# Ordering GpSimd's low parts behind VectorE's combinations in a differential-attention encoder layer

## The chip, the cores and the metric

The kernel runs on one core of one Trainium2 chip. The metric is the device time of one execution in microseconds. Times of the trace count from the start of the profiled span. The engines are TensorE (PE; its weight loads are PEld), VectorE (DVE), ScalarE (ACT), GpSimd (POOL) and SyncE (SP), which issues most transfers.

## The reference, cut to what matters

One layer of an encoder over 2048 positions of width 1024: a norm and one input projection, differential attention with 4 heads beside a recurrent group, an output projection, and a gated feed-forward part. The change touches the attention alone:

```python
sc = einsum('bqhcd,bkhcd->bhcqk', qb, kh) * scale        # c = 0, 1: two score maps per head, 64 wide
sc = sc - slopes[:, None, None, None] * dist              # distance bias
p = softmax(sc, axis=-1)
w = p[:, :, 0] - lam * p[:, :, 1]                         # the two maps are combined
o = einsum('bhqk,bkhe->bqhe', w, vh)                      # 128 wide values
o = rms_norm(o, subln_g) * (1.0 - lambda_init)
```

## The kernel before

Attention (`phase2`) runs over 4 heads of 16 query tiles, 128 queries each. One call of `step(n, cur)` (lines 550 to 597) issues the work of tile n (`cur`) together with later stages of earlier tiles: b1, b2 and b3 are tiles n-1, n-2 and n-3, and two tiles make a pair (`Pair`), whose stages come 4 (`pv`), 6 (`nrm`) and 8 (`fin`) steps behind its first tile. `nrm` and `fin` exist in even steps only. The order of instructions on TensorE, VectorE, ScalarE and GpSimd is the order in which `step` writes them (a manual schedule); each engine runs its queue in order.

In a step:

- `scores(hf)` (line 407): 12 matmuls into two PSUM tiles `sc`, one for each score map c, for half hf of the 2048 keys. The two tiles are used again by the next half.
- `biased(c, hf)` (line 411): VectorE's score pass, which adds the bias from PSUM to `e[c]` in SBUF and keeps the minimum. `softmax(c)` (line 416): ScalarE's exponential over 2048 columns.
- `combine(hf)` (line 427): VectorE's combination, e0 = e1 * rc + e0 over 1024 columns, both inputs in SBUF. There are two of these in a step.
- `transposed(i)` (lines 433, 442): TensorE turns a quarter of the combined tile (`tp`), ScalarE copies it to SBUF: quarter 0 to `wn`, quarter 1 to `wf`, quarters 2 and 3 to `wg`.
- `parts(i)` (line 448, by the helper `split`, lines 72 to 77): the fp32 values are split into a high part `wTh` (ScalarE, a rounding copy) and a low part `wTl` (GpSimd, value minus high part). `parts(1)` does `wf` (512 columns), `parts(2)` does `wg` (1024 columns).
- `values(part)` (lines 465 and 80 to 82): TensorE's products with the values, into `pv`. In an even step parts 0 and 1 of a pair, in an odd step parts 2 and 3. Part 0 uses `wn` alone, the others `wTh` and `wTl`.
- For the norm of a pair: with part 3 of the values ScalarE copies `pv` to `o` (line 472) and GpSimd squares it (`osq`, line 474) and the sums of the softmax (line 476). In the following even step TensorE adds the squares up (`norm_sums`, line 481, into `nrm_ps`), VectorE scales the sums (`norm_scale`, line 486), GpSimd takes a power and spreads it over 128 columns (`rr`, `rb`, lines 488 and 491). In the even step after that TensorE turns `rb` (`norm_spread`, line 497) and VectorE applies it (`scaled`, line 500).

In the last head GpSimd also makes low parts of the output weights (`load_out`, line 516), four times.

Of the kernel before, what the change touches and what calls it, by code (L numbers as in the profile page):

```python
# [9 lines left out]
F32 = mybir.dt.float32  # L10
# [3 lines left out]
AF = mybir.ActivationFunctionType  # L14
ALU = mybir.AluOpType
# [3 lines left out]
P = 128  # L19
# [10 lines left out]
EPS = 1e-6  # L30
# [12 lines left out]
def encoder_layer(ctx, tc, x, w_qkr, w_v, w_out, w_up, w_down, w_a, w_x, par, lams, g_attn, g_ffn, g_fin, out):  # L43
    nc = tc.nc
    V, A, G, T = nc.vector, nc.scalar, nc.gpsimd, nc.tensor

    def pool_of(name, **kw):
        return tc.tile_pool(name=name, reuse_waits="tile", **kw)
# [18 lines left out]
    mhalf = const.tile([P, 4], F32, name="mhalf")  # L67
# [4 lines left out]
    def split(hi, lo, src, hi_eng=A, lo_eng=V):  # L72
        if hi_eng is A:
            A.activation(out=hi, in_=src, func=AF.Copy)  # L74
        else:
            hi_eng.tensor_copy(hi, src)
        lo_eng.tensor_tensor(out=lo, in0=src, in1=hi, op=ALU.subtract)  # L77

    def mm3(ps, lh, ll, rh, rl, first, last):
        T.matmul(ps, lh, rh, start=first, stop=False)  # L80
        T.matmul(ps, lh, rl, start=False, stop=False)  # L81
        T.matmul(ps, ll, rh, start=False, stop=last)  # L82
# [243 lines left out]
    def phase2(kp):  # L326
        es = ExitStack()
        hip = es.enter_context(pool_of("ah", bufs=2))
        sm = es.enter_context(pool_of("asm", bufs=3))
# [10 lines left out]
        PQ = 2 * P  # L340
        NQ = 1

        ones = cp.tile([P, P], F32, name="ones")
# [15 lines left out]
                        op0=ALU.mult)  # L359
# [28 lines left out]
        class Tile:  # L388
# [35 lines left out]

            def combine(self, hf):
                e0, e1 = [e[:, hf * 1024:(hf + 1) * 1024] for e in self.e]
                V.scalar_tensor_tensor(out=e0, in0=e1, scalar=self.rc, in1=e0, op0=ALU.mult, op1=ALU.add)  # L427

            def transposed(self, i):

# [13 lines left out]
            def parts(self, i):  # L444

                j = self.t % 2
                dst = (slice(None), slice(0, 4) if i == 1 else slice(4, 12), slice(j * P, (j + 1) * P))
                split(self.pair.wh[dst], self.pair.wl[dst], self.wf if i == 1 else self.wg, lo_eng=G)

        class Pair:  # L450

# [8 lines left out]
            def values(self, part):  # L460
                if part == 0:
                    self.pv = ps_v.tile([P, PQ], F32, name="pv", tag="pv")
                for kt in range(part * 4, part * 4 + 4):
                    if part < NQ:
                        T.matmul(self.pv, self.vs[2][:, kt, :], self.wn[:, kt, :], start=kt == 0, stop=False)  # L465
                    else:
                        m = kt - 4 * NQ
                        mm3(self.pv, self.vs[0][:, kt, :], self.vs[1][:, kt, :], self.wh[:, m, :], self.wl[:, m, :],
                            kt == 0, kt == NT - 1)
                if part == 3:  # L470
                    self.o = sm.tile([P, PQ], F32, name="o", tag="o", bufs=3)
                    A.activation(out=self.o, in_=self.pv, func=AF.Copy)
                    self.sq = sm.tile([P, PQ], F32, name="osq", tag="osq", bufs=1)
                    G.tensor_tensor(out=self.sq, in0=self.o, in1=self.o, op=ALU.mult)
                    self.s2 = sm.tile([P, 2], F32, name="s2", tag="s2")
                    G.tensor_tensor(out=self.s2, in0=self.s0, in1=self.s0, op=ALU.mult)

            def norm_sums(self):
                self.ssp = nrm_ps[:, PQ:PQ + 4]
# [2 lines left out]

            def norm_scale(self):

                e0 = sm.tile([P, 2], F32, name="se", tag="se")
                V.scalar_tensor_tensor(out=e0, in0=self.s2, scalar=EPS * P, in1=self.ssp[:, 0:4:2], op0=ALU.mult, op1=ALU.add)
                r = sm.tile([P, 2], F32, name="rr", tag="rr")
                G.tensor_tensor(out=r, in0=e0, in1=mhalf[:, 0:2], op=ALU.pow)
                self.rb = sm.tile([P, 2, P], F32, name="rb", tag="rb", bufs=1)
                for j in range(2):  # L490
                    G.tensor_scalar(out=self.rb[:, j, :], in0=ones, scalar1=r[:, j:j + 1], scalar2=None, op0=ALU.mult)

            def norm_spread(self):

# [55 lines left out]
        def step(n, cur):  # L550

            b1 = tiles[n - 1] if 0 <= n - 1 < last else None
            b2 = tiles[n - 2] if 0 <= n - 2 < last else None
            pair = lambda lag: pairs[(n - lag) // 2] if n >= lag and (n - lag) // 2 < len(pairs) else None
            pv, nrm, fin = pair(4), pair(6), pair(8)
            if n % 2:
                nrm = fin = None
            b3 = tiles[n - 3] if 0 <= n - 3 < last else None
            if cur:
                cur.scores(0)  # L560
            if b1:
                b1.softmax(1)
            if cur:
                cur.biased(0, 0)
                cur.biased(1, 0)
            if b2:
                b2.transposed(0)
                b2.transposed(1)
                b2.parts(1)
            if b3:  # L570
                b3.parts(2)
            if pv:
                pv.values(n % 2 * 2)
            if fin:
                fin.norm_spread()
            if b1:
                b1.ratio()
                b1.combine(0)
            if cur:
                cur.scores(1)  # L580
                cur.biased(0, 1)
                cur.biased(1, 1)
            if b2:
                b2.transposed(2)
                b2.transposed(3)
            if cur:
                cur.softmax(0)
            if pv:
                pv.values(n % 2 * 2 + 1)
            if nrm:  # L590
                nrm.norm_sums()
            if b1:
                b1.combine(1)
            if fin:
                fin.scaled()
            if nrm:
                nrm.norm_scale()

        ordered = {mybir.EngineType.PE, mybir.EngineType.DVE, mybir.EngineType.Activation, mybir.EngineType.Pool}
        ks, vs = load_head(0)  # L600
# [13 lines left out]
        for h in range(NH):  # L614
            for t in range(NT):
                if t % 4 == 0:
                    qs = qs_next
                if t % 2 == 0:
                    pairs.append(Pair(h, t // 2, vs))
                tiles.append(Tile(h, t, qs, ks, pairs[-1]))  # L620
                step(n, tiles[n])
                if t % 4 == 1:
                    if t + 4 < NT:
                        qs_next = load_q(h, t // 4 + 1)
                    elif h + 1 < NH:
                        nxt = load_head(h + 1)
                        qs_next = load_q(h + 1, 0)
                        load_values(h + 1, nxt[1])
                if t == NT - 1 and h + 1 < NH:
                    sum_values(nxt[1])  # L630
                if h == NH - 1 and t in (6, 8, 10, 12):
                    raw = fetch_out(t // 2 + 1)
                if h == NH - 1 and t in (7, 9, 11, 13):
                    load_out(t // 2 + 1, t // 2 - 3, G, raw)
                n += 1
            if h + 1 < NH:
                ks, vs = nxt
# [3 lines left out]
        while n < last + 10:  # L641
            step(n, None)
            early.run(n - last)
            if n == last + 1:
                load_two((0, 1), (1, 2))
            if n == last + 4:
                load_two((2, 0), (3, 3))
            n += 1
# [671 lines left out]
    kp_stack = ExitStack()  # L1320
    kp = kp_stack.enter_context(pool_of("kp", bufs=2, side="right"))
    wo, x0 = phase2(kp)
    sl = Slots()
    sl.add(ctx.enter_context(pool_of("ba", bufs=1)), [f"b{i}" for i in range(9)])
# [75 lines left out]
```

## Time and profile before

| | |
|---|---|
| time, median of 3 runs | 2679.63 us (2678.31 to 2682.24) |
| profiled execution, its own time | 2677.01 us |
| its span | 2675.2 us |
| TensorE busy | 2580.4 us (96%) |
| VectorE busy | 1978.8 us (74%) |
| ScalarE busy | 1340.7 us (50%) |
| GpSimd busy | 574.9 us (21%) |
| mean granted clock of TensorE | 0.985 |

Busy shares are means over stages with different limits. Attention takes the span from about 520 to 1135 us; what bounds it is read from its own stretch, from the timelines of single engines and from the chain of work that ended last, in which each piece is followed back to what released it. TensorE's matmuls overlap in the timeline, and their ends are modelled; the chain shows them end to end. An operation of VectorE or GpSimd that is held shows as a longer record, not as idle time.

### The profile page before, as it was taken

The page shows a single profiled execution, that of the slowest core. Times are in us where ns is not written, and L with a number is a line of the kernel's source. Part 1 is how long each engine was busy: PE and PEld are TensorE (multiplying, and loading weights), DVE is VectorE, ACT ScalarE, POOL GpSimd, SP SyncE. Part 2 cuts the span into 40 slices and gives each one's busy share as a digit, 9 for nine tenths or more (in the row PEclk, how much of TensorE's full clock was granted, in tenths as well). Part 3 has the DMA queues.
Part 4 walks back from the last instruction along what each step waited for, and adds up shares of the span by engine and source line. Part 5 has one row for each costly group of instructions (what it writes and reads, how often), then busy time and mean ns, then how long its engine had stood idle before and what let it go on. Part 6 is the DMA issues. An engine that isn't in the chain of part 4 may idle for free.

```text
span 2675.2 us, 33375 instructions
## 1 busy us (share of the span) xinstructions
PE 2580.4 (96%) x12904; PEld 2098.3 (78%) x12904; DVE 1978.8 (74%) x2453; ACT 1340.7 (50%) x1730; POOL 574.9 (21%) x467
## 2 busy tenths in 40 slices
PE   8999999989999999999999999989999999899898
PEld 6878778768888888787778888878888877678686
DVE  5454554699999999644488888897777787765876
ACT  4343543678888888632344444454444453322432
POOL 1013313346666766700000000000000001000000
PEclk9999999989999999999999999999999999999999
DMA  5421221320202001344443434343333337554543
GB/s 190 129 85 60 81 79 64 130 93 17 87 23 87 25 25 38 99 149 138 169 165 118 154 122 143 129 161 126 123 122 124 115 108 177 130 147 98 148 144 126
DMA packets 141391, 297.60 MB, mean 111 GB/s; under 512 B 17904, under 2 KB 73968, under 8 KB 133552
## 3 DMA queue, kind: packets, MB, share of 16 engines
q1 hardware_dynamic: 134416, 272.55, 29.9%
q0 software_dynamic: 6240, 21.24, 4.2%
q8 instruction: 101, 1.65, 0.3%
q10 hardware_dynamic: 576, 1.69, 0.2%
q14 instruction: 58, 0.48, 0.1%
HBM read 177.98 MB, written 117.44 MB: 110 GB/s over the span
## 4 chain that ended last, share of the span: by engine, by line
PE 69%; DVE 6%; issue 2%; POOL 1%; ACT 1%; DMA 0%; POOLq 0%; SPq 0%; DVEq 0%; ACTq 0%
PE q L977 44%; PE sc L407 7%; PE tp L433 4%; PE po L82 2%; PE po L81 2%; PE po L80 2%; PE pv L465 2%; PE pv L81 2%; PE pv L80 2%; PE pv L82 2%; DVE e L411 1%; DVE u L992 1%; DVE wg L956 1%; PE nrm_ps L497 0%; POOL wTl L77 0%
## 5 line engine op out<-in xcount | busy, mean ns | idle before, releaser
L992 DVE TENSOR_TENSOR u<-q,u 128x512 f32<-128x512 f32 x340 | 234.6, 690 | 157.2 <-PE q L977 154.2
L951 ACT ACTIVATE wg<-sw 128x1024 fp32r<-128x1024 f32 (+1 forms) x136 | 140.7, 1034 | 408.5 <-PE q L977 222.9
L1252 POOL DMA_DIRECT2D x_d<-u x32 | 27.2, 851 | 1169.1 <-ACT u L999 904.3
L416 ACT ACTIVATE e<-e,mn 128x2048 f32<-128x2048 f32 x128 | 256.2, 2008 | 16.6 <-DVE mn L411 16.6
L407 PE MATMUL sc<-ks,qt 64*128 64x512 f32 x1536 | 233.9, 420 | 16.0 <-DVE mn L411 11.6
L1139 DVE SCALAR_TENSOR_TENSOR acc<-u,prm,acc 128x1023 f32<-128x1023 f32 (+1 forms) x176 | 226.0, 1284 | 7.2 <-ACT acc L1131 1.2
L427 DVE SCALAR_TENSOR_TENSOR e<-e,rc,e 128x1024 f32<-128x1024 f32 x128 | 214.3, 1675 | 2.3
L81 PE MATMUL ps<-hT_lo,wh 128*128 128x512 f32 x512 | 199.6, 390 | 0.0
L82 PE MATMUL ps<-hT_hi,wl 128*128 128x512 f32 x512 | 199.6, 390 | 0.0
L80 PE MATMUL ps<-hT_hi,wh 128*128 128x512 f32 x512 | 199.4, 390 | 0.0
L407 PEld LDWEIGHTS sc<-ks,qt 64*128 64x128 f32 x1536 | 147.2, 189 | 62.3 <-DVE mn L411 20.0
L956 DVE TENSOR_TENSOR wg<-sw,wg 128x1024 fp32r<-128x1024 f32 (+1 forms) x136 | 161.9, 1190 | 28.4 <-ACT wg L951 28.2
L956 DVE TENSOR_TENSOR wg<-wr,wg 128x512 fp32r<-128x512 f32 (+3 forms) x136 | 126.9, 933 | 67.6 <-ACT wg L951 67.6
L951 ACT ACTIVATE wg<-wr 128x512 fp32r<-128x512 f32 (+3 forms) x136 | 111.7, 822 | 117.6 <-PE q L977 106.2
L411 DVE CUSTOM_DVE_ANT_0 e<-sc,strip,mn 128x1024 f32<-128x1024 f32 x128 | 159.1, 1281 | 14.5 <-PE sc L407 11.8
L977 PE MATMUL q<-b12r,wg 128*128 128x512 f32 x472 | 162.2, 397 | 2.1 <-ACT wg L951 1.4
L977 PE MATMUL q<-b14r,wg 128*128 128x512 f32 x464 | 160.2, 397 | 2.9 <-ACT u L999 2.9
L977 PE MATMUL q<-b0r,wg 128*128 128x512 f32 x472 | 162.3, 398 | 0.0
L977 PE MATMUL q<-b1r,wg 128*128 128x512 f32 x472 | 160.6, 394 | 1.2 <-DVE b1r L777 1.2
L77 POOL TENSOR_TENSOR wTl<-wg,wTh 128x1024 fp32r<-128x1024 f32 x64 | 157.2, 2456 | 0.0
L411 DVE CUSTOM_DVE_ANT_0 e<-sc,strip 128x1024 f32<-128x1024 f32 x128 | 150.9, 1213 | 8.4 <-PE sc L407 8.3
L77 POOL TENSOR_TENSOR wTl<-wf,wTh 128x512 fp32r<-128x512 f32 x64 | 127.9, 1998 | 111.5 <-ACT wTh L74 108.9
(301 smaller groups left out, 6524.3 us busy)
## 6 DMA issues: line engine op xcount, KB each, us to landing
wr<-in_w_up_dram SPq DMA_DIRECT2D x66, 512.0 KB, 5.5
s_d<-sw SPq DMA_DIRECT2D x22, 1024.0 KB, 4.8
sw<-s_d SPq DMA_DIRECT2D x22, 1024.0 KB, 4.8
a_d<-acc SPq DMA_DIRECT2D x154, 128.0 KB, 1.9
x_d<-u POOLq DMA_DIRECT2D x32, 512.0 KB, 5.5
wr<-a_d SPq DMA_DIRECT2D x32, 512.0 KB, 4.7
xt<-in_x_dram SPq DMA_DIRECT2D x30, 512.0 KB, 4.9
ws<-in_w_qkr_dram SPq DMA_DIRECT2D x16, 512.0 KB, 3.2
```

Source lines behind the costliest of these rows:

```text
L77: lo_eng.tensor_tensor(out=lo, in0=src, in1=hi, op=ALU.subtract)
L80: T.matmul(ps, lh, rh, start=first, stop=False)
L81: T.matmul(ps, lh, rl, start=False, stop=False)
L82: T.matmul(ps, ll, rh, start=False, stop=last)
L407: T.matmul(self.sc[c][:, n * CH:(n + 1) * CH], l[rows, q], r[rows, kk], start=i == 0, stop=i == 2)
L411: V.tensor_tensor_reduce(out=self.e[c][:, hf * 1024:(hf + 1) * 1024], in0=self.sc[c], in1=strip[:, off:off + 1024], scale=SLOPES[self.h], ...
L416: A.activation(out=self.e[c], in_=self.e[c], func=AF.Exp, scale=-1.0, bias=self.mn[:, 2 * c + 1:2 * c + 2], accum_out=self.s[c])
L951: A.activation(out=hi, in_=src, func=AF.Copy)
L956: V.tensor_tensor(out=lo, in0=src, in1=hi, op=ALU.subtract)
L977: T.matmul(ps, l, r[:, k, :], start=new is not None and k == 0 and n == 0, stop=k == m - 1 and n == 2, skip_group_check=True)
L992: V.tensor_tensor(out=out, in0=a, in1=b_, op=ALU.add)
L1139: V.scalar_tensor_tensor(out=acc[:, 0:n], in0=u[:, o + tap:o + tap + n], scalar=prm[:, C_FW + 3 * m + tap:C_FW + 3 * m + tap + 1], in1=acc ...
```

## The change

Four things are changed in attention, and nothing else:

- In a step, `parts(2)` of tile n-3 is written ahead of `parts(1)` of tile n-2, and `parts(1)` is written behind the first combination.
- The low part of `wg` is made to wait for the second combination that was written last (that of the step before), the low part of `wf` for the first combination of its own step. Both waits are dependencies between engines that no data asks for.
- The squares (`osq` and the square of the softmax sums) move from the odd step, with the copy of `o`, to the following even step, behind the low part of `wf`.
- The power and the spreading of the norm (`rr`, `rb`) move from the even step, with `norm_scale`, to the following odd step, behind the low part of `wf`.

```diff
             def combine(self, hf):
-                V.scalar_tensor_tensor(out=e0, in0=e1, scalar=self.rc, in1=e0, op0=ALU.mult, op1=ALU.add)
+                return V.scalar_tensor_tensor(out=e0, in0=e1, scalar=self.rc, in1=e0, op0=ALU.mult, op1=ALU.add)
...
             def parts(self, i):
-                split(self.pair.wh[dst], self.pair.wl[dst], self.wf if i == 1 else self.wg, lo_eng=G)
+                src = self.wf if i == 1 else self.wg
+                A.activation(out=self.pair.wh[dst], in_=src, func=AF.Copy)
+                return G.tensor_tensor(out=self.pair.wl[dst], in0=src, in1=self.pair.wh[dst], op=ALU.subtract)
...
                 if part == 3:
                     self.o = sm.tile([P, PQ], F32, name="o", tag="o", bufs=3)
                     A.activation(out=self.o, in_=self.pv, func=AF.Copy)
-                    self.sq = sm.tile([P, PQ], F32, name="osq", tag="osq", bufs=1)
-                    G.tensor_tensor(out=self.sq, in0=self.o, in1=self.o, op=ALU.mult)
-                    self.s2 = sm.tile([P, 2], F32, name="s2", tag="s2")
-                    G.tensor_tensor(out=self.s2, in0=self.s0, in1=self.s0, op=ALU.mult)
+
+            def squares(self):
+                self.sq = sm.tile([P, PQ], F32, name="osq", tag="osq", bufs=1)
+                self.s2 = sm.tile([P, 2], F32, name="s2", tag="s2")
+                G.tensor_tensor(out=self.s2, in0=self.s0, in1=self.s0, op=ALU.mult)
+                return G.tensor_tensor(out=self.sq, in0=self.o, in1=self.o, op=ALU.mult)
...
+            def norm_rows(self):
                 r = sm.tile([P, 2], F32, name="rr", tag="rr")
...
-            pv, nrm, fin = pair(4), pair(6), pair(8)
+            pv, nrm, fin, row = pair(4), pair(6), pair(8), pair(7)
             if n % 2:
                 nrm = fin = None
+            else:
+                row = None
...
                 b2.transposed(1)
-                b2.parts(1)
             if b3:
-                b3.parts(2)
+                after(b3.parts(2), "second")
...
                 b1.ratio()
-                b1.combine(0)
+                marks["first"] = b1.combine(0)
+            if b2:
+                after(b2.parts(1), "first")
             if cur:
                 cur.scores(1)
                 cur.biased(0, 1)
                 cur.biased(1, 1)
+            if nrm:
+                nrm.squares()
+            if row:
+                row.norm_rows()
...
             if b1:
-                b1.combine(1)
+                marks["second"] = b1.combine(1)
...
+        def after(ins, mark):
+            if mark in marks:
+                tc.add_manual_dep(ins.ins, marks[mark].ins.name,
+                                  mybir.DependencyInfo(mybir.DependencyClass.Sync, mybir.DependencyReason.SCHED_ONLY),
+                                  reason="shared access to SBUF")
```

GpSimd's queue over one pair of steps in the middle of attention, before: the squares of a finished pair, the low parts of the even step, the rows of the norm, the low parts of the odd step (`s` is the softmax sums).

```order
L474 TENSOR_TENSOR osq<-o 128x256
L476 TENSOR_TENSOR s_4624<-s_4010 128x2
L77 TENSOR_TENSOR wTl<-wf,wTh 128x4x128
L77 TENSOR_TENSOR wTl<-wg,wTh 128x8x128
L488 TENSOR_TENSOR rr<-se,mhalf 128x2
L491 TENSOR_SCALAR rb<-ones,rr 128x128 x2
L77 TENSOR_TENSOR wTl<-wf,wTh 128x4x128
L77 TENSOR_TENSOR wTl<-wg,wTh 128x8x128
```

The same queue after, from the start of an even step:

```order
L450 TENSOR_TENSOR wTl<-wg,wTh 128x8x128
L450 TENSOR_TENSOR wTl<-wf,wTh 128x4x128
L479 TENSOR_TENSOR s_4697<-s_4010 128x2
L480 TENSOR_TENSOR osq<-o 128x256
L450 TENSOR_TENSOR wTl<-wg,wTh 128x8x128
L450 TENSOR_TENSOR wTl<-wf,wTh 128x4x128
L494 TENSOR_TENSOR rr<-se,mhalf 128x2
L496 TENSOR_SCALAR rb<-ones,rr 128x128 x2
```

In the even step the squares moved from the front of the two low parts to behind them; in the odd step the rows of the norm did the same, and `wg` comes ahead of `wf`. TensorE's queue keeps its order, with the sums of the squares (line 481) behind part 1 of the values and ahead of the next step's scores.

ScalarE's queue between two copies of a step, where the high parts stand (lines with - before, with + after):

```order
 L442 ACTIVATE wTn<-tp 128x4x128
 L442 ACTIVATE wf<-tp 128x512
-L74 ACTIVATE wTh<-wf 128x4x128
-L74 ACTIVATE wTh<-wg 128x8x128
+L449 ACTIVATE wTh<-wg 128x8x128
+L449 ACTIVATE wTh<-wf 128x4x128
 L442 ACTIVATE wg<-tp 128x512 x2
```

Only the two high parts changed places.

## Rows read from the trace of the kernel before

**Rows 1.** Stretch table: us, busy of PE, PEld, DVE, ACT, POOL (instructions), clock, DMA, GB/s.

```profile
700.00:800.00 100.00, 100.00 (x749) 83.41 (x749) 96.75 (x148) 87.69 (x120) 68.45 (x52) 1.00 0.14 46
```

**Rows 2.** Chain that ended last, 782 to 836 us: shares by line; then start, us, what.

```profile
by line: PE sc L407 37.0%; PE tp L433 24.6%; PE pv L465 9.6%; PE pv L81 8.3%; PE pv L80 8.2%; PE pv L82 8.1%; PE nrm_ps L497 2.5%; PE nrm_ps L481 1.9%
...
810.65 1.60 PE sc L407 x10
...
815.45 1.59 PE sc L407 x12
...
819.50 0.34 PE nrm_ps L481 x4
819.84 1.59 PE sc L407 x12
...
823.90 1.86 PE sc L407 x12
...
828.23 1.60 PE sc L407 x10
```

**Rows 3.** VectorE's timeline: start, us, engine, line, operation [idle before <- releaser].

```profile
812.67 1.21 DVE L411 CUSTOM_DVE_ANT_0 e<-sc,strip 128x1024 f32<-128x1024 f32 x1
...
815.40 1.29 DVE L427 SCALAR_TENSOR_TENSOR e<-e,rc,e 128x1024 f32<-128x1024 f32 x1
817.08 1.28 DVE L411 CUSTOM_DVE_ANT_0 e<-sc,strip,mn 128x1024 f32<-128x1024 f32 x1 [0.39 <-PE sc L407]
...
819.49 1.81 DVE L427 SCALAR_TENSOR_TENSOR e<-e,rc,e 128x1024 f32<-128x1024 f32 x1
...
821.68 1.21 DVE L411 CUSTOM_DVE_ANT_0 e<-sc,strip 128x1024 f32<-128x1024 f32 x1
...
828.02 2.30 DVE L427 SCALAR_TENSOR_TENSOR e<-e,rc,e 128x1024 f32<-128x1024 f32 x1
```

**Rows 4.** GpSimd's timeline of the same pair of steps.

```profile
812.29 0.93 POOL L474 TENSOR_TENSOR osq<-o 128x256 f32<-128x256 f32 x1 [0.63 <-ACT o L472]
...
815.91 1.92 POOL L77 TENSOR_TENSOR wTl<-wf,wTh 128x512 fp32r<-128x512 f32 x1 [1.30 <-ACT wTh L74]
817.78 2.43 POOL L77 TENSOR_TENSOR wTl<-wg,wTh 128x1024 fp32r<-128x1024 f32 x1
...
822.66 1.19 POOL L491 TENSOR_SCALAR rb<-ones,rr 128x128 f32<-128x128 f32 x2
...
826.79 2.45 POOL L77 TENSOR_TENSOR wTl<-wg,wTh 128x1024 fp32r<-128x1024 f32 x1
```

**Rows 5.** ScalarE's timeline of the even step.

```profile
814.56 0.61 ACT L442 ACTIVATE wf<-tp 128x512 f32<-128x512 f32 x1
815.20 0.63 ACT L74 ACTIVATE wTh<-wf 128x512 fp32r<-128x512 f32 x1
815.74 1.05 ACT L74 ACTIVATE wTh<-wg 128x1024 fp32r<-128x1024 f32 x1
817.73 1.09 ACT L442 ACTIVATE wg<-tp 128x512 f32<-128x512 f32 x2 [0.94 <-PE tp L433]
```

**Rows 6.** Timeline of the last head: meetings of the two engines, and osq alone.

```profile
1036.54 2.38 POOL L77 TENSOR_TENSOR wTl<-wg,wTh 128x1024 fp32r<-128x1024 f32 x1
1036.63 3.37 DVE L427 SCALAR_TENSOR_TENSOR e<-e,rc,e 128x1024 f32<-128x1024 f32 x1
...
1043.68 0.61 POOL L474 TENSOR_TENSOR osq<-o 128x256 f32<-128x256 f32 x1 [4.76 <-ACT o L472]
...
1073.88 1.31 POOL L77 TENSOR_TENSOR wTl<-wf,wTh 128x512 fp32r<-128x512 f32 x1 [0.43 <-ACT wTh L74]
1074.01 2.26 DVE L427 SCALAR_TENSOR_TENSOR e<-e,rc,e 128x1024 f32<-128x1024 f32 x1
...
1075.12 3.42 POOL L77 TENSOR_TENSOR wTl<-wg,wTh 128x1024 fp32r<-128x1024 f32 x1
```

**Rows 7.** Stretch table, ten us of the last head (columns of rows 1).

```profile
1040.00:1050.00 10.00, 8.03 (x54) 6.30 (x55) 8.72 (x14) 8.25 (x11) 4.89 (x5) 1.00 0.17 54
```

More of the change, by code (lines that the diff above doesn't have):

```diff
@@ L483, in norm_scale @@
             def norm_scale(self):
-                e0 = sm.tile([P, 2], F32, name="se", tag="se")
-                V.scalar_tensor_tensor(out=e0, in0=self.s2, scalar=EPS * P, in1=self.ssp[:, 0:4:2], op0=ALU.mult, op1=ALU.add)
+                self.se = sm.tile([P, 2], F32, name="se", tag="se")
+                V.scalar_tensor_tensor(out=self.se, in0=self.s2, scalar=EPS * P, in1=self.ssp[:, 0:4:2], op0=ALU.mult, op1=ALU.add)
+            def norm_rows(self):
                 r = sm.tile([P, 2], F32, name="rr", tag="rr")
-                G.tensor_tensor(out=r, in0=e0, in1=mhalf[:, 0:2], op=ALU.pow)
+                G.tensor_tensor(out=r, in0=self.se, in1=mhalf[:, 0:2], op=ALU.pow)
                 self.rb = sm.tile([P, 2, P], F32, name="rb", tag="rb", bufs=1)
-                for j in range(2):
-                    G.tensor_scalar(out=self.rb[:, j, :], in0=ones, scalar1=r[:, j:j + 1], scalar2=None, op0=ALU.mult)
+                return [G.tensor_scalar(out=self.rb[:, j, :], in0=ones, scalar1=r[:, j:j + 1], scalar2=None, op0=ALU.mult)
+                        for j in range(2)]
             def norm_spread(self):
@@ L597, in step @@
                 nrm.norm_scale()
+        marks = {}
+        def after(ins, mark):
[3 more added lines that the diff above has]
+                                  reason="shared access to SBUF")
         ordered = {mybir.EngineType.PE, mybir.EngineType.DVE, mybir.EngineType.Activation, mybir.EngineType.Pool}
```

## The prediction, made before the changed kernel had run

> **What bounds the kernel now.** I read the table of stretches first. The change touches only attention, and one 100 us stretch of it stands for four alike: TensorE 100% busy, VectorE 97%, ScalarE 88%, GpSimd 68%, granted clock 1.00 [rows 1]. Two engines are nearly full, so busy shares can't say which of them sets the pace; the chain does. Over three pairs of steps every piece of it is TensorE's [rows 2]. A pair runs from 810.65 to 828.23, 17.6 us. Its four blocks of scores take 1.60, 1.59, 1.59 and 1.86 us [rows 2]: the only visible stall in a pair is 0.27 us in the last of them. The reader should take one more thing from these rows: the sums of squares for the norm (nrm_ps from osq) start at 819.50, and the odd step's scores stand right behind them in TensorE's queue, at 819.84.
>
> Next VectorE's timeline. A combination that meets nothing takes 1.28 us; the second one of an even step takes 1.81 and of an odd step 2.30 [rows 3]. GpSimd's timeline says why: a low part of 2.43 or 2.45 us, begun earlier, ends inside each of them (817.78 to 820.21, 826.79 to 829.24) [rows 4]. So 0.53 + 1.02 = 1.55 us a pair of VectorE's time is blocking, which is what the change is aimed at. But it hardly reaches TensorE: in the even step VectorE is idle for 0.39 us before its next score pass, waiting for scores [rows 3]. Only the 0.53 us in the even step arrive, as a late first score pass of the odd step (821.68), and end as the 0.27 us stall.
>
> The Trainium skill, page "SBUF — State Buffer", section "Who interferes with whom", says that a VectorE instruction with two SBUF inputs and a GpSimd instruction that reads SBUF exclude each other for a whole instruction and that the one that started first has it. The rows agree (2.30 against 1.28). By that rule with VectorE as the bound, all 1.55 us a pair would come back; by the chain at most 0.27.
>
> **The change, part by part.** I count from the even step's first scores (810.65 = 0). The pattern repeats in 29 even steps (6 to 62) that still have scores and a norm.
>
> *The upside.* If the second combination of the even step is no longer blocked, the stall shrinks from 0.27 to about 0.05: 0.2 us a pair.
>
> *ScalarE.* The high part of wg now goes ahead of that of wf. Before, both start when wf is there, 815.17 [rows 5]. So wg's is ready at 815.17 + 1.05 = 816.22, or +5.57, and wakes GpSimd 0.08 us later (815.83 to 815.91) [rows 4, 5]: +5.65. ScalarE's total is unchanged and costs nothing.
>
> *The waits.* That of wg's low part is for the second combination of the previous step, which is over before this step's first score pass (812.67) [rows 3]: free. That of wf's low part is for this step's first combination (815.40, to about +5.95) [rows 3]; it too is met by the time that wg's low part is done. What stands behind it in GpSimd's queue is the point: the squares in even steps, the norm's rows in odd ones.
>
> *The squares.* Before, osq runs at 812.29 (+1.64), ahead of both low parts, and its reader comes at +8.85 [rows 2, 4]: 6 us to spare. Now it is last. The first combination holds wg's low part until +5.95; 2.4 us [rows 4] make +8.35; wf's low part, 1.31 us alone [rows 6], +9.6. The second combination has wanted to start since 819.49 (+8.84) [rows 3] and is blocked by it. At +9.6 it and the squares both want SBUF. One row shows such a meeting: at 1074.01 a combination waited for a low part, the next low part was already queued, and the combination went first (2.26 us, the queued one 3.42) [rows 6]. So the combination runs to +10.7, osq takes 0.61 us alone [rows 6]: +11.3, and with the wake-up the sums start at +11.4 in place of +8.85. TensorE stands for **2.5 us** in every even step, with the odd step's scores queued behind. Lower bound: no blocking at all, 5.65 + 2.43 + 1.31 + 0.61 + 0.08 = +10.1, a stall of 1.2 us. Even that is not hidden, since every term is a queue order or a duration of the trace. Upper bound: as under rival B, 2.5 + 2.1. I take 2.5, as the order of the meeting has a row.
>
> *The norm's rows* move from the even step's end to the odd step's end, behind its wf low part. The odd step's scores now end near +13.4; its first combination holds wg's low part until 4 us later, and 2.4 and 1.3 us of low parts follow: +21. Two rb take 1.19 us [rows 4], the power in front, 128x2, under 1 us (an estimate, from 0.61 us for 256 columns): +23. Their reader in the next pair, the spreading, stands in front of its second scores (815.45, +4.8 of a pair, now near +24) [rows 2]. Hidden with a margin of about 1 us; if that cover goes, the excess adds one for one.
>
> *Odd steps.* wg's low part, then wf's: wf's now runs into the second combination there as well, for about 1 us, but the next scores absorb that as they absorb the 1.02 us now.
>
> *Sum.* 2.5 - 0.2 = 2.3 us a pair, times 29 = 67 us. In four pairs of the last head the low parts of output weights share GpSimd; there the kernel before has itself a combination of 3.37 us [rows 6] and loses time that the new order partly avoids; I take off 1 us for each. 67 - 4 = **+63 us**. Start and drain of attention have the same work on GpSimd, which I cost at nothing, give or take 4 us. The profiled run took 2677.0 us, its span 2675.2; the median 2679.6 lies 2.6 us above, and I split that: 2678 + 63 = 2741.
>
> **Rivals.**
>
> *B, GpSimd wins the race in odd steps.* After the stall ScalarE and VectorE both start fresh from the odd step's first scores, so two ready times can be compared. From a score pass to the first combination: 815.40 - 812.67 = 2.73 us [rows 3]. From a score pass to wg's low part: copies start 0.65 us behind it (817.73 against 817.08) [rows 3, 5], two copies take 0.97 to the next start, then 1.05 and 0.08: 2.75 us. The combination leads by 0.02 us, nearly a tie. If GpSimd goes first, the combination is held for 2.1 us, as at 1036.63, where wg's low part had started 0.09 us ahead (3.37 - 1.28) [rows 6], and the next scores with it: 29 x 2.1 = 61 us more, 2802. For it: the margin is under every jitter. Against it: the same sign in each pair.
>
> *C, the squares slip in ahead of the waiting combination.* Then the sums start at about +10.4, 1 us sooner: 63 - 29 = +34, 2712. Against it: the one meeting of [rows 6] went the other way.
>
> *D, faster.* The stall never forms and the 0.27 us come back: 29 x 0.27 = 8 us, 2670. It decides at +8.85: wf's low part would have to end by +8.1 where I find +9.6 (+9.4 without any blocking), so ScalarE's high part of wg would have to come over a microsecond earlier. It stands behind the copy of wf, so nothing in the rows makes it. Were VectorE the bound, as its 97% suggest, 29 x 1.55 = 45 us would return, 2633; the chain of TensorE alone speaks against it. The page named above, by its lock rule, would give that figure if VectorE's time were the kernel's.
>
> *E, the change doesn't do what it says, and nothing shows.* It is true that wf's low part moves from the first combination to the second, so the blocking mostly stays; for no difference the squares would have to be early too. 2678.
>
> *F, the clock.* If the granted clock fell in the new stalls, TensorE would lose more. A stretch with 8.03 of 10 us busy kept 1.00 [rows 7]; the new pair would be busy 17.3 of 19.9 us.
>
> **How the numbers follow.** Forecast (DVE first at both meetings) 0.47; B or a mixture of it 0.29; C 0.13; D 0.04; E 0.03; F or another worse one 0.04. The likeliest gives 2741. The range of 8 in 10 takes in C at its low end and B at its high end, each with some 5 us for start and drain: 2706 to 2807; the forecast's own is 2730 to 2752. A difference of 0.2% (5 us) is about what a measurement of this kernel can tell: faster 0.04, same 0.03, slower 0.93.
>
> **What would show it.** Right: pairs of about 19.9 us; TensorE idle for 2.4 us ahead of the sums (nrm_ps from osq), released by GpSimd's osq, 29 times; second combinations still near 1.8 and 2.2 us. B: first combinations of odd steps of 3.4 us and pairs near 22 us. C: osq ahead of the end of the even step's second combination, and pairs near 18.9 us. Wrong: sums that start right behind the values, all combinations at 1.28 us, and pairs of 17.3 us.

## The result, and the profile after

| | before | after |
|---|---|---|
| time, median | 2679.01 us (2678.31 to 2682.24, 4 runs) | 2796.65 us (2795.69 to 2797.18, 4 runs) |
| ratio after to before | | 1.0431, 95% interval 1.0418 to 1.0444 |
| span of the profiled execution | 2675.2 us | 2794.9 us |
| mean granted clock | 0.985 | 0.967 |

The change costs 117.6 us. That is slower, as forecast, and inside the range, but 56 us above the forecast of 2741. Counted from the first combination of one pair of steps to that of the next, the first two pairs of attention are unchanged (35.1 us both), the 25 in the middle go from 438.8 to 538.9 us (17.55 to 21.56 a pair), and the four of the last head from 76.1 to 93.3. That is 100.1 + 17.2 = 117.3 us: all of it lies in pairs of steps.

The stretch table, in the stretch and with the columns of [rows 1]:

```profile
700.00:800.00 100.00, 86.15 (x606) 71.29 (x605) 78.74 (x121) 70.42 (x97) 57.02 (x42) 0.95 0.12 39
```

TensorE fell from 100% to 86%, and its granted clock from 1.00 to 0.95. TensorE's waits, longest first (what waited, for whom: us in total, times, longest):

```profile
PE nrm_ps L485 <- POOL osq L480: 63.6, 30, 3.3
...
PE sc L407 <- DVE mn L411: 16.5, 23, 1.5
```

The first is all but new: before, the sums of squares waited for GpSimd's `osq` once, for 0.9 us, in the drain of attention. Now they do so in each of 29 pairs as well, 62.7 us more. The second was 11.6 us before. So waits explain 63 + 5 of the 118 us, and something else must account for the other 50.

One even step shows the wait. GpSimd's timeline (columns of [rows 3]; `s` is the squared softmax sums):

```profile
806.21 2.41 POOL L450 TENSOR_TENSOR wTl<-wg,wTh 128x1024 fp32r<-128x1024 f32 x1 [3.15 <-ACT wTh L449]
808.59 1.29 POOL L450 TENSOR_TENSOR wTl<-wf,wTh 128x512 fp32r<-128x512 f32 x1
809.85 0.19 POOL L479 TENSOR_TENSOR s<-s 128x2 f32<-128x2 f32 x1
810.00 1.59 POOL L480 TENSOR_TENSOR osq<-o 128x256 f32<-128x256 f32 x1
```

VectorE's timeline of the same step and the next:

```profile
805.08 1.28 DVE L427 SCALAR_TENSOR_TENSOR e<-e,rc,e 128x1024 f32<-128x1024 f32 x1
...
809.75 1.36 DVE L427 SCALAR_TENSOR_TENSOR e<-e,rc,e 128x1024 f32<-128x1024 f32 x1
...
814.88 1.23 DVE L411 CUSTOM_DVE_ANT_0 e<-sc,strip 128x1024 f32<-128x1024 f32 x1 [2.00 <-PE sc L407]
...
821.87 1.67 DVE L427 SCALAR_TENSOR_TENSOR e<-e,rc,e 128x1024 f32<-128x1024 f32 x1
```

TensorE's timeline, the score and transpose blocks of the even step's second half and the odd step's first:

```profile
805.64 1.66 PE L407 MATMUL sc<-ks,qt 64*128 64x512 f32 x12
807.24 1.09 PE L433 MATMUL tp<-ident,e 128*128 128x128 f32 x8
...
811.64 0.61 PE L485 MATMUL nrm_ps<-ones,osq 128*128 128x2 f32 x4 [1.89 <-POOL osq L480]
812.17 2.68 PE L407 MATMUL sc<-ks,qt 64*128 64x512 f32 x12
814.79 1.62 PE L433 MATMUL tp<-ident,e 128*128 128x128 f32 x8
```

`osq` runs 1.59 us instead of 0.61 [rows 6], because the second combination (809.75 to 811.11) goes first. TensorE stands for 1.89 us, and then the same twelve score matmuls take 2.68 us instead of 1.66, the same eight transposes 1.62 instead of 1.09. Stretches of 1 us (columns of [rows 1]) show why:

```profile
811.00:812.00 1.00, 0.36 (x4) 0.36 (x4) 0.11 (x1) 1.00 (x1) 0.58 (x1) 1.00 0.00 0
812.00:813.00 1.00, 1.00 (x9) 0.85 (x10) 0.55 (x2) 0.97 (x2) 0.00 (x0) 0.75 0.00 0
813.00:814.00 1.00, 1.00 (x8) 0.83 (x6) 0.00 (x0) 0.00 (x0) 0.00 (x0) 0.50 0.02 8
814.00:815.00 1.00, 1.00 (x6) 0.35 (x4) 0.12 (x1) 0.00 (x0) 0.00 (x0) 0.50 0.45 131
815.00:816.00 1.00, 1.00 (x6) 1.00 (x6) 1.00 (x1) 0.06 (x1) 0.00 (x0) 0.55 0.00 0
816.00:817.00 1.00, 1.00 (x11) 1.00 (x10) 1.00 (x3) 1.00 (x3) 0.00 (x0) 1.00 0.08 16
```

The granted clock, last but two, falls to 0.50 (1.2 GHz) behind the hole and is back at 1.00 some 3 us later (in seven of the pairs some 7 us later). The slower blocks alone are 1.02 + 0.53 = 1.55 us.

Not all holes do this. Stretches of 4 us, beginning behind the sums of four pairs:

```profile
705.00:709.00 4.00, 4.00 (x34) 3.31 (x33) 2.91 (x7) 1.77 (x3) 0.00 (x0) 1.00 0.11 33
769.37:773.37 4.00, 4.00 (x33) 3.31 (x32) 2.90 (x7) 2.15 (x5) 0.00 (x0) 1.00 0.11 33
...
812.24:816.24 4.00, 4.00 (x22) 3.05 (x21) 1.91 (x5) 1.04 (x3) 0.00 (x0) 0.57 0.14 39
833.47:837.47 4.00, 4.00 (x18) 2.96 (x19) 1.32 (x3) 0.66 (x2) 0.00 (x0) 0.50 0.12 37
```

Of the 29 holes in steady work, 24 look like the last two and five like the first two. The five came after waits of 2.74, 2.22, 2.14, 2.15 and 2.21 us, not shorter than the 1.89 us at 811.64. And it is in exactly those five pairs that the odd step's first combination took 3.44 us; the timeline of all engines at the second of them:

```profile
773.73 2.40 POOL L450 TENSOR_TENSOR wTl<-wg,wTh 128x1024 fp32r<-128x1024 f32 x1 [5.01 <-DVE rc L423]
773.76 3.45 DVE L427 SCALAR_TENSOR_TENSOR e<-e,rc,e 128x1024 f32<-128x1024 f32 x1
```

This is rival B: GpSimd started 0.03 us before the combination and held it. In this kernel VectorE lost the race of the odd step behind each hole that kept the clock and won it behind each of the other 24. My reading is that a fallen clock delays the transposes, and with them ScalarE's copies, more than the scores; the third experiment has exceptions. A pair whose hole kept the clock, up to the lost race, takes 20.1 us (one of the five 20.6), most of those with a fallen clock 21.8, and the four in the middle that begin with a lost race 21.9 to 22.4.

### The profile page after: what moved, and what is told of

It is laid out like the page before. It is cut to its first block, busy times and chain, and to the rows that moved or that the text cites. A ratio compares the mean times of both kernels' runs of the same rounds, so it can differ in the third digit from the quotient of the medians.

```text
span 2794.9 us, 33412 instructions
## 1 busy us (share of the span) xinstructions
PE 2631.8 (94%) x12904; PEld 2136.8 (76%) x12904; DVE 1963.3 (70%) x2453; ACT 1340.7 (48%) x1730; POOL 583.5 (21%) x467
## 4 chain that ended last, share of the span: by engine, by line
PE 51%; DVE 5%; issue 2%; POOL 2%; ACT 1%; DMA 0%; SPq 0%; POOLq 0%; DVEq 0%; ACTq 0%
PE q L999 42%; PE po L82 2%; PE po L81 2%; PE po L80 2%; PE sc L407 1%; POOL wTl L450 1%; DVE wg L978 1%; PE tp L433 1%; DVE u L1014 1%; PE tp L740 0%; ACT e L416 0%; DVE acc L1161 0%; POOL s L479 0%; POOL osq L480 0%; PE nrm_ps L485 0%
## 5 line engine op out<-in xcount | busy, mean ns | idle before, releaser
L407 PE MATMUL sc<-ks,qt 64*128 64x512 f32 x1536 | 256.6, 456 | 20.9 <-DVE mn L411 16.5
L450 POOL TENSOR_TENSOR wTl<-wg,wTh 128x1024 fp32r<-128x1024 f32 x64 | 173.4, 2710 | 267.9 <-ACT wTh L449 242.9
L407 PEld LDWEIGHTS sc<-ks,qt 64*128 64x128 f32 x1536 | 163.8, 207 | 66.9 <-DVE mn L411 26.4
L427 DVE SCALAR_TENSOR_TENSOR e<-e,rc,e 128x1024 f32<-128x1024 f32 x128 | 190.1, 1486 | 2.3
L433 PEld LDWEIGHTS tp<-ident,e 128*128 128x128 f32 x1024 | 123.8, 153 | 52.6 <-issue 39.0
```

Of the source, the lines that this page charges most:

```text
L407: T.matmul(self.sc[c][:, n * CH:(n + 1) * CH], l[rows, q], r[rows, kk], start=i == 0, stop=i == 2)
L450: return G.tensor_tensor(out=self.pair.wl[dst], in0=src, in1=self.pair.wh[dst], op=ALU.subtract)
```

## The experiments

**1. Squares back, all else as after.**

```diff
                     A.activation(out=self.o, in_=self.pv, func=AF.Copy)
+                    self.squares()
...
-            if nrm:
-                nrm.squares()
```

> The changed kernel with one thing undone: the two squares stand again where the kernel before has them, behind the copy of o in the odd step, so that GpSimd does them ahead of the next even step's low parts. The added waits, the order of the low parts, and the later place of the norm's rows stay. Theory 1 (the late squares hold TensorE, and the clock falls in that hole): sums of squares start right behind part 1 of the values, TensorE idles on osq for under 5 us in all, granted clock 1.00 in steady attention, 2665 to 2685 us. Theory 2 (the waits and the order of the low parts cost it): still over 2750 us.

Measured: 2698.29 us, ratio 1.0067 (1.0053 to 1.0080). The wait for `osq` is gone (0.9 us once), the steady pairs are back at 17.55, and the clock is 1.00 there. So 98 of the 118 us hang on the squares. But 18 us stay, 13 us above the upper end of what I expected. In the profiled execution 8.3 us of them lie in the middle (each of three changes of head has one pair of 20.6 us) and 7.7 in the last head. GpSimd's timeline at the first of these changes:

```profile
672.45 1.19 POOL L497 TENSOR_SCALAR rb<-ones,rr 128x128 f32<-128x128 f32 x2
673.61 0.19 POOL L480 TENSOR_TENSOR s<-s 128x2 f32<-128x2 f32 x1
673.75 0.61 POOL L481 TENSOR_TENSOR osq<-o 128x256 f32<-128x256 f32 x1
674.32 1.30 POOL L377 TENSOR_TENSOR vn<-vt 128x512 f32<-128x512 f32 x1
675.57 3.38 POOL L450 TENSOR_TENSOR wTl<-wg,wTh 128x1024 fp32r<-128x1024 f32 x1
```

The norm's rows, the squares and the next head's values (`vn`) now stand in one unbroken row, and the low part of `wg` behind them starts straight after, with no idle time ahead of it.

**2. Squares alone:** the kernel before, with only the squares moved behind the low parts.

```diff
             if cur:
                 cur.scores(1)
                 cur.biased(0, 1)
                 cur.biased(1, 1)
+            if nrm:
+                nrm.squares()
```

> The kernel before with one thing done: the two squares are written in the even step behind its low parts (which keep their old order, wf then wg, and get no waits). Theory 1: osq comes behind wg's low part, which ends near +9.6 us of a pair, and behind or ahead of the blocked combination, so the sums wait 1.5 to 2.6 us in each of 29 pairs and the clock falls as in the changed kernel: 2745 to 2810 us. Theory 2: within 10 us of 2679.

Measured: 2794.4 us, ratio 1.0429 (1.0407 to 1.0450), mean clock 0.966. This one move alone costs what the whole change costs, though not in the same parts: the waits for `osq` come to 51.6 us in 24 pairs, those for the scores' buffers to 25.7 us.

**3. The change without its two waits.**

```diff
-            if mark in marks:
+            if False:
```

> The changed kernel without the two added waits; all queues keep the changed order. Theory 1: the waits are met before they are asked for in nearly every step, so 2787 to 2807 us. Theory 2: back towards 2680 to 2720 us.

Measured: 2793.72 us, ratio 1.0429 (1.0412 to 1.0445). The waits, which are what the change is named for, cost nothing and bring nothing that shows in the time. They do touch the race: here VectorE lost it 8 times, twice behind a hole that kept the clock, but six times behind a hole where the clock had fallen. The stretch of 4 us behind the sums of one of these six, and its combination on VectorE's timeline:

```profile
1023.02:1027.02 4.00, 4.00 (x23) 2.97 (x24) 1.66 (x3) 0.96 (x3) 0.00 (x0) 0.64 0.11 33
...
1028.65 3.48 DVE L427 SCALAR_TENSOR_TENSOR e<-e,rc,e 128x1024 f32<-128x1024 f32 x1
```

So a fallen clock doesn't settle the race by itself.

**4. Order and waits only:** the change, with squares and norm's rows both at their old places.

```diff
+                    self.squares()
...
-            if nrm:
-                nrm.squares()
-            if row:
-                row.norm_rows()
...
             if nrm:
                 nrm.norm_scale()
+                nrm.norm_rows()
```

> The changed kernel with squares and norm's rows both at their old places, so that only the order of the two low parts and the added waits are left of the change. If e1's 3 us at each change of head come from the rows that stand ahead of the values' sum there, they go: within 6 us of before in the first three heads, 2675 to 2690 us. If they come from the low parts' order: 2693 to 2700 us as e1.

Measured: 2678.89 us, ratio 0.9999 (0.9990 to 1.0008). The middle takes 438.6 us, the last head 77.4. So the 18 us left over in the first experiment belong to the norm's rows. GpSimd's timeline at the same change of head:

```profile
671.63 1.27 POOL L377 TENSOR_TENSOR vn<-vt 128x512 f32<-128x512 f32 x1
674.45 2.81 POOL L450 TENSOR_TENSOR wTl<-wg,wTh 128x1024 fp32r<-128x1024 f32 x1 [1.55 <-ACT wTh L449]
```

`vn` is over early, and the low part waits 1.55 us for its data instead of for the queue. Nor does the new order keep the engines apart. The combinations' group on the page (count, busy, mean ns), of the kernel before and of this one:

```profile
L427 DVE SCALAR_TENSOR_TENSOR e<-e,rc,e 128x1024 f32<-128x1024 f32 x128 | 214.3, 1675 | 2.3
...
L427 DVE SCALAR_TENSOR_TENSOR e<-e,rc,e 128x1024 f32<-128x1024 f32 x128 | 214.8, 1678 | 2.3
```

The mean is 1678 ns against 1675. The meeting has moved from one low part to another and is as long as it was.

**5. No meeting at all:** the kernel before, with the low parts written as zeros, so that GpSimd reads nothing there. The writes need no high part either, so they also come earlier, and they are shorter.

```diff
-                split(self.pair.wh[dst], self.pair.wl[dst], self.wf if i == 1 else self.wg, lo_eng=G)
+                A.activation(out=self.pair.wh[dst], in_=self.wf if i == 1 else self.wg, func=AF.Copy)
+                G.memset(self.pair.wl[dst].bitcast(F32), 0.0)
```

> The kernel before with GpSimd's low parts replaced by writing zeros: the low parts are left out of the result, and GpSimd reads nothing while the combinations run, so the two can't meet over reads of SBUF. What the meeting is worth at most. If TensorE's chain sets the pace: all combinations near 1.28 us, pairs of 17.3 to 17.5 us, 2666 to 2677 us. If VectorE's blocked 1.55 us a pair were on the path: 2630 to 2645 us.

Measured: 2671.31 us, ratio 0.9971 (0.9961 to 0.9980). The combinations' group on the page:

```profile
L427 DVE SCALAR_TENSOR_TENSOR e<-e,rc,e 128x1024 f32<-128x1024 f32 x128 | 164.8, 1288 | 2.3
```

VectorE gets back 214.3 - 164.8 = 50 us of its time, and the kernel 8 to 9. This bounds what freeing the combinations by any order of the low parts could have brought. It also places it: the 25 middle pairs gain only 1.6 us together, the last head 5.8.

**6. Another use of the same idea:** the kernel before, with VectorE's scaling of the finished pair (`scaled`, line 500) moved from behind the second combination to behind the first, where VectorE idles (0.39 us in [rows 3]).

```diff
                 b1.combine(0)
+            if fin:
+                fin.scaled()
...
                 b1.combine(1)
-            if fin:
-                fin.scaled()
```

> The kernel before with VectorE's scaling of o (0.4 us) moved from behind the second combination of the even step to behind the first, where VectorE waits 0.39 us for scores anyway; GpSimd's work is untouched. If the 0.27 us stall comes from the late first score pass of the odd step: pairs shorter by 0.15 to 0.25 us, 2672 to 2677 us. If not: no difference.

Measured: 2670.3 us, ratio 0.9970 (0.9959 to 0.9981): a little faster than both kernels, and 2 us below the range that I expected. VectorE's timeline:

```profile
799.71 1.68 DVE L427 SCALAR_TENSOR_TENSOR e<-e,rc,e 128x1024 f32<-128x1024 f32 x1
...
801.67 1.23 DVE L411 CUSTOM_DVE_ANT_0 e<-sc,strip 128x1024 f32<-128x1024 f32 x1 [0.21 <-PE sc L407]
...
808.13 2.17 DVE L427 SCALAR_TENSOR_TENSOR e<-e,rc,e 128x1024 f32<-128x1024 f32 x1
...
814.16 0.47 DVE L500 SCALAR_TENSOR_TENSOR o<-o,gsub,nrm_ps 128x256 f32<-128x256 f32 x1
```

The combinations are blocked nearly as before (1.68, 2.17 against 1.81, 2.30), and yet the score pass behind the first of them now waits 0.21 us for its scores: VectorE is ahead. Again the middle gains little (437.0 against 438.8 us, 0.07 a pair, where I expected 0.15 to 0.25) and the last head more (72.1 against 76.1).

**7. and 8. The hole filled.** To see the stall without the clock, sixteen matmuls that nobody reads stand ahead of the sums of squares. In the seventh kernel they read the pair's high parts, in the eighth only the head's values:

```diff
             def norm_sums(self):
+                for i in range(16):
+                    T.matmul(nrm_ps[:, PQ + 8:PQ + 8 + 248], self.vs[0][:, 4, :], self.wh[:, 0, 0:248], start=True, stop=True)
...
+                for i in range(16):
+                    T.matmul(nrm_ps[:, PQ + 8:PQ + 8 + 248], self.vs[0][:, 4, :], self.vs[0][:, 5:7, 0:124], start=True, stop=True)
```

> The changed kernel with 16 idle-time matmuls of 248 columns (0.12 us each, 1.9 us) on TensorE ahead of the sums of squares in each even step, into columns of nrm_ps that nobody reads. They fill most of the hole without shortening it. If the fall of the granted clock behind the hole costs what the trace suggests (about 16% of 560 us at half rate, some 45 us), the clock stays at 1.00 and the time is 2745 to 2765 us although TensorE has more to do. If the clock costs nothing: 2790 to 2805 us.

> The changed kernel with 16 matmuls of 248 columns (0.12 us each, 1.9 us together) on TensorE ahead of the sums of squares of each even step, from the head's values into columns of nrm_ps that nobody reads; unlike those of e4 they read nothing that ScalarE has to write again, so they hold nobody up. They fill most of the hole and don't shorten it. If the fall of the granted clock behind the hole is a cost of its own: clock 1.00 in steady attention, the score blocks of odd steps back at 1.6 to 1.9 us, 2745 to 2765 us. If it costs nothing: 2790 to 2805 us.

Measured: 2873.14 us, ratio 1.0721 (1.0704 to 1.0738), and 2815.35 us, ratio 1.0512 (1.0497 to 1.0526). Both miss. The seventh built a wait of its own; ScalarE's waits:

```profile
ACT wTh L449 <- PE nrm_ps L484: 148.2, 27, 5.9
```

The next high part needs the buffer that the fillers read, so everything behind it came later (the waits for `osq` grew to 86.8 us). It says nothing about the clock. The eighth did keep the clock behind the sums. TensorE's waits there:

```profile
PE sc L407 <- DVE mn L411: 53.5, 69, 1.8
...
PE nrm_ps L487 <- POOL osq L480: 2.5, 3, 0.9
```

The hole is gone, but another is in its place. The timeline of all engines in an odd step:

```profile
820.32 2.39 POOL L450 TENSOR_TENSOR wTl<-wg,wTh 128x1024 fp32r<-128x1024 f32 x1 [6.86 <-DVE rc L423]
820.35 3.44 DVE L427 SCALAR_TENSOR_TENSOR e<-e,rc,e 128x1024 f32<-128x1024 f32 x1
```

Now 29 of 29 first combinations of the odd steps are held to 3.44 us, the next scores wait for their buffers (in two pieces, 0.9 and 0.7 us), and in about half of the pairs (15 times) the clock falls behind that wait instead (in the pair before this one to 0.65 in the stretch from 804 to 805 us and to 0.50 in the next two). So with the clock kept behind the sums the race was lost every time, as the five pairs of the changed kernel had suggested.

**9. and 10. No race, with the hole and with the hole filled.** To take the race out, the low part of `wg` waits for the first combination of its own step; the tenth kernel adds the filler of the eighth.

```diff
-            if b3:
-                after(b3.parts(2), "second")
...
                 marks["first"] = b1.combine(0)
+            if b3:
+                after(b3.parts(2), "first")
```

> The changed kernel with one thing added: wg's low part waits for the first combination of its own step (not for the second of the step before), so GpSimd can't start it ahead of that combination in odd steps. The few pairs of the changed kernel in which it did (a combination of 3.4 us, 5 of 29, 2.1 us each) should go, the hole ahead of the sums and the clock's fall behind it stay: 2780 to 2792 us, clock 0.97.

> e9 with e5's 16 filling matmuls in the hole. Here neither the race nor the clock should cost anything, and only the late squares are left: pairs of 19.9 us, clock 1.00 in steady attention, 2735 to 2750 us, as the prediction's likeliest case. The difference to e9 is then the clock's price, some 40 us. If the clock's fall costs nothing, e10 is no faster than e9. If the filling itself costs time, as in e5, it is over 2790 us, with first combinations at 1.28 us.

Measured: 2803.96 us, ratio 1.0460 (1.0443 to 1.0478), and 2779.53 us, ratio 1.0362 (1.0333 to 1.0390). Neither has a combination over 3 us. Both came out above what I expected, since the wait makes the low parts later and the hole longer. TensorE's waits in the ninth:

```profile
PE nrm_ps L485 <- POOL osq L480: 77.7, 30, 4.5
```

and in the tenth:

```profile
PE nrm_ps L487 <- POOL osq L480: 34.0, 29, 2.7
```

The comparison is what counts. In the middle a pair takes 21.93 us in the ninth and 20.69 in the tenth, though TensorE loses more in the tenth: 34.0/29 = 1.2 us of hole and some 1.9 us of filler, 3.1 in all, against 77.7/30 = 2.6. Above the old 17.55 the tenth has 3.14 us, just its hole and filler; the ninth has 4.38, 1.8 us more than its hole. (The holes of the 25 middle pairs alone are 1.0 and 2.4 us on the mean; by them the tenth has 0.2 us left over and the ninth 1.9.) The clock fell behind 21 of these 25 holes in the ninth and behind 2 in the tenth. One-us stretches behind a sum of squares in the ninth:

```profile
793.00:794.00 1.00, 1.00 (x6) 0.98 (x6) 0.00 (x0) 0.92 (x2) 0.00 (x0) 0.50 0.00 0
794.00:795.00 1.00, 1.00 (x6) 0.81 (x8) 0.55 (x2) 0.00 (x0) 0.00 (x0) 0.50 0.00 0
```

and in the tenth:

```profile
803.00:804.00 1.00, 0.68 (x6) 0.67 (x8) 0.00 (x0) 0.30 (x2) 0.26 (x1) 1.00 0.00 0
804.00:805.00 1.00, 1.00 (x10) 0.81 (x12) 0.55 (x2) 0.00 (x0) 0.00 (x0) 1.00 0.00 0
```

I put the extra 1.8 us a pair down to the clock, at 0.50 against 1.00; it is close to the 21.8 - 20.1 = 1.7 us between pairs of the changed kernel with a fallen and a kept clock.

## Why the prediction was right, and where it was too low

*The bound and the upside.* Right. TensorE's chain sets the pace: with all meetings gone 50 us of VectorE's time came back and 9 us of the kernel's, so the rival in which VectorE's 97% is the bound (2633) falls. The Trainium skill, page "SBUF — State Buffer", section "Who interferes with whom", says that the one that issued first has the shared access for its whole instruction, and that a GpSimd instruction that only writes doesn't contend. Runs here agree with both: 0.03 us of a lead cost the combination 2.17 us (3.45 - 1.28), and in the fifth experiment 36 of the 128 combinations ran beside a write of zeros for 0.1 us or more, and none of these took over 1.29 us. Smaller than I said was the stall of 0.27 us in a steady pair: what is to be had there is 0.07 us (17.55 to 17.48), and most of the rest lies in the last head. The size for rival D, 8 us, was right for a partly wrong reason.

*The waits, ScalarE, the odd steps' second combination.* At nothing, and nothing it was (experiments 3 and 4).

*The squares.* Right to within 0.1 us up to the sums, counted from the first combination of the even step (805.08; in the prediction +4.75):

| | predicted | measured |
|---|---|---|
| low part of `wg` starts | +1.20 | +1.13 |
| low part of `wf` ends | +4.85 | +4.80 |
| `osq` ends | +6.55 | +6.51 |
| sums of squares start | +6.65 | +6.56 |

VectorE went first at both meetings of this step, as forecast. But one of my signs failed: the second combinations were to stay near 1.8 and 2.2 us, and here they take 1.36 and 1.67. Over all of attention the page of the changed kernel has

```profile
L427 DVE SCALAR_TENSOR_TENSOR e<-e,rc,e 128x1024 f32<-128x1024 f32 x128 | 190.1, 1486 | 2.3
```

so that VectorE got 214.3 - 190.1 = 24 us back, which brought nothing, since TensorE's chain sets the pace. The hole is 2.2 us on the mean (62.7/29), under the 2.5 I gave, since TensorE's own queue stands later against VectorE's: the second scores start 0.56 us behind the first combination (805.64 - 805.08), before 0.05 [rows 2, 3]. But the whole pair with a kept clock takes 20.1 us, 2.55 more than before, where I had 2.3 and "about 19.9".

*The clock, rival F: the step that failed.* I gave it 0.04 on the strength of one row of the last head, 8.03 of 10 us busy at 1.00 [rows 7], and it happened in 24 of 29 pairs. That row holds most of one hole of 1.90 us, behind which the clock stayed. The trace of the kernel before has one more hole of this length, in the drain of attention, and I didn't read it. TensorE's timeline and the stretch behind each of the two:

```profile
1041.26 0.50 PE L407 MATMUL sc<-ks,qt 64*128 64x512 f32 x1 [1.90 <-DVE mn L411]
1041.26:1045.26 4.00, 3.29 (x22) 2.40 (x23) 3.67 (x6) 4.00 (x5) 1.40 (x3) 1.00 0.02 4
...
1106.24 0.58 PE L81 MATMUL pv<-wTl,vt 128*128 128x256 f32 x1 [2.06 <-POOL wTl L77]
1107.00:1108.00 1.00, 1.00 (x7) 1.00 (x6) 1.00 (x1) 0.29 (x1) 1.00 (x2) 0.50 1.10 397
```

Behind the second the clock was 0.50, and eight transposes took 1.91 us (from 1106.62) where the next eight took 1.04 (from 1110.00). So the rows held one case for each outcome, and no ground for 0.04. The sum had the clock's price at nothing; it should have had a bound for it: one score block and one block of transposes at double length, 1.6 + 1.1 us more a pair. At 1.7 us a pair, 20 of the 25 middle pairs make 34 of their 100 us; 25 x 2.55 = 64 are the forecast's mechanism, and some 2 are left.

*The race, rival B.* Its ready times were right to a few hundredths of a us ("nearly a tie", 0.02 us; the rows have 0.03 the other way), but it is no independent case, for it hangs together with the clock. VectorE lost 5 of 5 where the clock stayed and 29 of 29 in the eighth kernel; where the clock fell it won 24 of 24 here, and 19 of 25 in the third experiment. So the fallen clock mostly helps VectorE, but isn't all that decides. And the race hardly adds up here: a pair in the middle that begins with a lost race is at most 0.6 us longer than its neighbours, not 2.1. That the total came out near B's 2802 is coincidence; its 61 us were to come from the race, and most of the 56 us above the forecast came with the clock.

*The last head.* Too low: I put 4 x (2.3 - 1) = 5 us, it was 17.2. There the holes are longer (2.58 to 3.32 us), the clock fell in all four, and a pair is still 1.5 us longer than one in the middle (23.3 against 21.8), as it was before (19.0 against 17.55): I had hoped for part of that back.

*The norm's rows.* "Hidden with a margin of about 1 us" held in steady pairs. It failed where GpSimd has more to do, at the three changes of head and in the last head: 2698.29 against 2678.89 is 19 us when the squares stay in place. In the changed kernel itself this can't be told apart from the squares' price. I had looked at one steady pair only.

*Open.* The price of the clock is known from two comparisons (1.7 and 1.8 us a pair) in which other things move by some tenths. Why five holes, longer than most of the others, kept the clock at 1.00, as one of the two holes in the kernel before did, is not settled.

## What to carry to other kernels

Before putting an operation behind others in a queue, look for its reader: here a 0.6 us square that had 6 us to spare became the last thing that the fullest engine waited for. An engine's blocked time is worth only what reaches the chain; a kernel that leaves the cause out altogether (experiment 5) gives the ceiling of a change in one run. And cost a new hole of some 2 us on TensorE at more than its length: look in the trace at hand for every hole of that size and at the clock behind each, not at one of them. Last, walk the order through the irregular places (changes of head, the last head) as well as a steady pair.

## What the hardware showed that I had not expected

- Behind a hole of 1.9 us on TensorE the granted clock was 0.50 for some 3 us, with TensorE busy up to the hole and behind it. By the two comparisons above that cost 1.7 to 1.8 us, nearly the hole again.
- Five holes of 2.1 to 2.7 us in the same kernel kept 1.00, and in the tenth kernel fillers and then a hole of 1.41 us (to 803.32) did too. In the eighth, two waits of 0.9 and 0.7 us, 0.5 us apart, were followed by a fall to 0.50 in 15 pairs.
- In the changed kernel the winner of a race between VectorE and GpSimd went with TensorE's clock (5 of 5 against 24 of 24). The likely way is by the transposes, whose copies GpSimd's part needs; that is argued and not shown, and without the added waits six races were lost behind a fallen clock.
